# Gating one step ahead, taps behind the key chains, context's parts first: a reordering in a two-layer diffusion trunk

## The chip, the cores and the metric

The kernel runs on one core of a Trainium2 chip. A core has TensorE (PE: matmuls, and the loads of their weights, PEld), VectorE (DVE), ScalarE (ACT), GpSimd (POOL) and SyncE (SP, which here only issues DMAs). The metric is the device time of one execution in microseconds (us); lower is better.

## The reference, cut to what matters

A stream of 256 latent tokens and a prefix of 256 context tokens, width 1024, pass through two layers. All is float32. What the change touches is the first half of a layer, the token mixing:

```python
h = modulate(rmsnorm(x, norm1_g[l]), sh1, sc1)           # and hc likewise for the context
p = h @ w_in[l]                                          # GLU | q k v | gates, one projection
# (a) convolution branch
u = a * sigmoid(g)                                       # a, g: halves of the GLU columns
u = silu(layernorm(dwconv1d(u, conv_dw, conv_dw_b)))     # depthwise, 31 taps, 512 channels
y_conv = u @ w_conv_out
# (b) attention: 8 heads of 64; q, k of latents are rotated (rope);
#     each latent reads a window of the 4 x 64 grid (with a learned bias) and all context keys;
#     context tokens read context tokens only
y_attn = merge_heads(attention(q, k, v, k_ctx, v_ctx, rpb)) @ w_na_out
# (c) gates
x = x + g1 * ((sigmoid(gc) * y_conv + sigmoid(ga) * y_attn) @ w_out)
```

The second half is a gated MLP with a convolution of width 3. In the second (last) layer the context gives only keys and values.

## The kernel before

Activations lie with channels on the 128 partitions and tokens along the free axis: 512 columns in the first layer (256 latents, 256 context), 256 in the last. A matmul in full float32 precision is made of three: weights and activations are each split into a high part in a faster format (float32r) and the rest, and high x high, high x low, low x high are summed (`mm3`, L197 to L199). A `group` is one output tile of 128 channels: 8 input tiles x 3 = 24 matmuls of 512 columns in the first layer. Its weights come by one DMA of 512 KB on SP's queue, are split by ACT (the high part, L216), and get their low part either from ACT (L217) and an accumulating DMA of POOL (L218), or from DVE (L168).

The order of the work is written by hand as the order of the calls; a planner then orders each engine's queue, taking what is ready by its own estimate of durations, earlier calls first. `tc.issue_after(i)` keeps what is called inside behind `i` on the same engine. Beside the main order run *side* generators. `group` calls `slot()` in its middle and at its end, and each slot lets every side generator do one step:

- `conv_run` issues `rate` taps of the depthwise convolution. A tap (L673; L671 for a channel tile's first) is one DVE instruction over 128 channels and all columns, `cb = u * w + cb`. There are 4 channel tiles x 31 taps; a tile's taps can start once its GLU is done (`glu`: tanh on ACT, L691, then the product on DVE, L693). If `after[0]` is set, taps called later stand behind that instruction on DVE.
- `Attention.run` makes a step of the attention every few slots: products of queries and keys (L495), scores (DVE, L516: bias and row maximum; it sets `after[0]`), exponential and division (ACT, L519 and L522; DVE, L521), the turning of the probabilities (PE, L561; ACT copies, L564 and L567) and their product with the values (PE, L578; ACT and DVE, L595 and L596).
- later `ada_dots` (L304): products of the modulation weights on DVE, with weights by DMA into memory that the attention had used before.

The heads go in four pairs, j = 0 to 3. `qk(j)` makes the queries' and keys' groups of a pair; behind each, a chain of DVE and ACT rotates the latents' part (L859 to L869) and splits all parts into high (ACT, L881) and low (DVE, L882). `glu_groups(j)` makes the two groups of channel tile j of the GLU. In the first layer they alternate:

```python
qk(0)
...
for j in range(1, 4):
    glu_groups(j)
    qk(j)
    rate[0] = 3
```

and then gates (one group each) are made while attention is still busy, at most five. PSUM has four banks for groups (`main`), two (`sc`) and one and one (`pt`, `po`) for the attention. After the attention comes the LayerNorm of the convolution (`layer_norm`: what is left of the taps, five a slot, then sums L949 to L951 and a matmul, L955), the other gates, the two branch projections with their merge (L993, L998 to L1001), and the output projection.

Of the kernel before, what the change touches and what calls it, by code (L numbers as in the profile page):

```python
# [19 lines left out]
S = 256  # L20
GW = 64
# [32 lines left out]
def trunk(ctx: ExitStack, tc: tile.TileContext, xt, cvec, crow, wall, wada, params, bias_t, rope_t, out):  # L54
    nc = tc.nc
    pe, act, dve, pool, sp = nc.tensor, nc.scalar, nc.vector, nc.gpsimd, nc.sync
# [11 lines left out]
    def nm(s):  # L68
        uid[0] += 1
        return f"{s}_{uid[0]}"  # L70
# [18 lines left out]
    def add_side(gen):  # L89
        side.append(gen)  # L90
# [541 lines left out]
    for l in range(DEPTH):  # L632
        last = l == DEPTH - 1
        NS = 1 if last else 2
        T = NS * S
        ALL = slice(0, T)

        with ExitStack() if last else start as e1a:
# [59 lines left out]
            def in_group(t, c, tag="main"):  # L698
                return group(psum(tag), unit8(l, U_IN + t), *h1, c)

            def glu_groups(j):
                pa = in_group(T_GLU + 2 * (j - 1), ALL)
                pg = in_group(T_GLU + 2 * (j - 1) + 1, ALL)
                copied = None if last else att.ahead(j - 2)
                with tc.issue_after(copied.ins) if copied else ExitStack():
                    glu(j, pa, pg)

# [5 lines left out]
            with ExitStack() as e1b:  # L713
# [5 lines left out]
                def keep_v(t, ps):  # L719
                    if t > 1:  # L720
                        act.copy(halves(V[t - 2]), back(ps))
                        return
                    v = tmp()
                    act.copy(halves(v), back(ps))
                    for b in range(NB_):
                        for r in range(2):
                            at = r * GW + BASE[b]
                            sp.dma_start(VW[2 * t + r :: ROWS, b], v[at : at + WC])  # L728
# [108 lines left out]
                    glu_groups(1)  # L837

                conv = conv_run()
                rate[0] = 3 if last else 2.0  # L840
                add_side(conv)

                def qk(j):

                    att.ahead(j - 2)
                    bt = eb.tile([P, 5, NS_ // 2], F32, tag="bias", bufs=2 if last else 1, name=nm("bias"))
                    both = []
                    for what in range(2):
# [10 lines left out]
                        dve.tensor_tensor(part(r1[:, LAT]), lat, part(rope[:, 0, :]), ALU.mult)  # L859
                        dve.stream_shuffle(part(r2[:, LAT]), lat, SWAP16)  # L860
                        dve.tensor_tensor(r2[:, LAT], r2[:, LAT], rope[:, 1, :], ALU.mult)
                        if what == 0:
                            rq = tmp()
                            dve.tensor_tensor(
                                rq[:, LAT].rearrange("p (b r c) -> p b r c", b=NB_, r=ROWS),
                                blocks(r1[:, LAT]), blocks(r2[:, LAT]), ALU.add,
                            )
                        else:
                            dve.tensor_tensor(r1[:, LAT], r1[:, LAT], r2[:, LAT], ALU.add)  # L869
                        f = eb.tile([P, 2, KN if what else w], F32R, tag="qk"[what], bufs=2, name=nm("qk"))  # L870
                        if what == 0:
                            to = [([f[:, a, LAT] for a in range(2)], rq[:, LAT])]
                            if T > S:
                                to.append(([f[:, a, CTX] for a in range(2)], ctx_))
                        else:
                            rv_ = r1[:, LAT].rearrange("p (r c) -> p r c", r=ROWS)
                            to = [([f[:, a, KCTX] for a in range(2)], ctx_)]
                            for d, c in ((slice(0, KL), slice(GW - TC, GW)), (slice(KX, KN), slice(0, TC))):
                                to.append(([f[:, a, d].rearrange("p (c r) -> p r c", r=ROWS) for a in range(2)], rv_[:, :, c]))
                        for (hi, lo), src in to:  # L880
                            act.activation(hi, src, AF.Identity, scale=sc)  # L881
                            end = dve.scalar_tensor_tensor(lo, src, sc, hi.bitcast(F32), ALU.mult, ALU.subtract)  # L882
                        both.append(f)
                    att.pair(j, *both, bt, end)

                if l == 0:
                    for t in range(4):
                        keep_v(t, pv[t])
                    qk(0)
                    arun = att.run()  # L890
                    add_side(arun)
                    for j in range(1, 4):
                        glu_groups(j)
                        qk(j)
                        rate[0] = 3
                else:
                    glu_groups(2)
                    rate[0] = 3
                    wvs = [wunit(l, U_V + uu) for uu in range(4)]
                    for half in range(2):  # L900
                        pv = {t: psum() for t in (2 * half, 2 * half + 1)}
                        for k in range(KD):
                            v_tile(pv, wvs[k // 2], k, pv)
                            if k % 2:
                                slot()
                        for t, p in pv.items():
                            keep_v(t, p)
                    qk(0)
                    glu_groups(3)
                    arun = att.run()  # L910
                n = 0
                if last:
                    add_side(arun)
                    for j in range(1, 4):
                        gate(ea, n)
                        n += 1
                        qk(j)
                while att.busy() and n < (14 if last else 5):
                    gate(ea, n)
                    n += 1  # L920
                while att.busy():
# [435 lines left out]
```

## Time and profile before

| | |
|---|---|
| median of 3 runs | 1056.0 us (1055.9 to 1057.1) |
| the profiled execution | 1054.6 us, its span 1052.8 us |
| PE busy | 1032.4 us (98%) |
| DVE busy | 893.2 us (85%) |
| ACT busy | 565.6 us (54%) |
| POOL busy | 43.7 us (4%) |
| granted clock of TensorE | 0.997 of full speed |

The profile is of one execution. Times of rows are from the first instruction's start; "busy" of PE is modelled from pipelined matmuls. A row of waits says which engine's instruction waited for which, the total, how many times and the longest. A row of the timeline has the start, the duration, the engine and the line, the operation, what it writes and reads, how many instructions are merged, and in brackets the idle time before it and what ended that.

### The profile page before, as it was taken

What the parts mean: (1) busy time and instruction counts of PE and PEld (TensorE: products, weight loads), DVE (VectorE), ACT (ScalarE), POOL (GpSimd) and SP (SyncE); (2) the same over time, 40 slices, a digit from 0 to 9 for tenths busy, and PEclk for the clock granted to TensorE, in tenths of its full rate; (3) what the DMA queues carried; (4) which work ended last, traced back from release to release, by engine and by line L of the source; (5) the groups of instructions that cost most, each with busy time, mean ns of one, the idle gap of its engine ahead of it and who ended that gap; (6) DMA issues with size and microseconds to landing.
All of it is one profiled execution on the core that took longest, in us unless ns stands there. A gap on an engine that the chain in (4) does not pass through costs nothing.

```text
span 1052.8 us, 17991 instructions
## 1 busy us (share of the span) xinstructions
PE 1032.4 (98%) x6886; PEld 932.9 (89%) x6886; DVE 893.2 (85%) x1608; ACT 565.6 (54%) x921; POOL 43.7 (4%) x59
## 2 busy tenths in 40 slices
PE   9999999999999999999999999999999999999997
PEld 7787788888889988888888889999889999999996
DVE  6568899999998787878788888799899988988883
ACT  4458768545434644444444223545777666766652
POOL 1111110011000000000000000000000000000000
PEclk9999999999999999999999999999999999999998
DMA  9989674888945345454545887556734485666781
GB/s 374 305 221 229 156 181 121 258 255 236 305 146 177 104 140 160 140 164 143 166 145 160 301 289 249 180 189 209 208 123 135 161 292 176 193 201 199 221 283 57
DMA packets 59511, 209.26 MB, mean 199 GB/s; under 512 B 7201, under 2 KB 7457, under 8 KB 59425
## 3 DMA queue, kind: packets, MB, share of 16 engines
q1 hardware_dynamic: 54384, 190.77, 55.3%
q0 software_dynamic: 4752, 17.30, 8.7%
q8 instruction: 54, 0.88, 0.3%
q14 instruction: 33, 0.26, 0.1%
q10 hardware_dynamic: 288, 0.04, 0.0%
HBM read 187.63 MB, written 1.05 MB: 179 GB/s over the span
## 4 chain that ended last, share of the span: by engine, by line
PE 68%; DVE 17%; ACT 5%; DMA 4%; issue 3%; SPq 1%; DVEq 0%; ACTq 0%
PE main L197 20%; PE main L198 20%; PE main L199 20%; DVE cb L673 6%; PE main L736 4%; DVE wlo L168 3%; DMA raw<-in_wall 2%; DVE t L304 2%; DMA own<-in_wada 1%; SPq L728 1%; PE sc L197 1%; PE sc L199 1%; PE sc L198 1%; DVE qk L882 1%; ACT pp L519 1%
## 5 line engine op out<-in xcount | busy, mean ns | idle before, releaser
L197 PE MATMUL main<-h,whi 128*128 128x256 f32 (+1 forms) x1328 | 433.1, 326 | 1.2 <-DVE qk L882 1.2
L198 PE MATMUL main<-h,whi 128*128 128x256 f32 (+1 forms) x1328 | 430.2, 324 | 0.9 <-DVE h L1001 0.7
L199 PE MATMUL main<-h,wlo 128*128 128x256 f32 (+1 forms) x1328 | 429.9, 324 | 1.2 <-DVE wlo L168 1.1
L167 ACT CAST whi<-raw 128x1024 fp32r<-128x1024 f32 (+1 forms) x211 | 218.3, 1039 | 234.8 <-PE main L198 173.6
L168 DVE TENSOR_TENSOR wlo<-raw,whi 128x1024 fp32r<-128x1024 f32 (+1 forms) x211 | 253.6, 1208 | 67.2 <-ACT whi L167 66.4
L197 PEld LDWEIGHTS main<-h,whi 128*128 128x128 f32 x1328 | 252.8, 190 | 22.0 <-issue 1.3
L199 PEld LDWEIGHTS main<-h,wlo 128*128 128x128 f32 x1328 | 252.5, 190 | 18.5 <-DVE wlo L168 1.8
L198 PEld LDWEIGHTS main<-h,whi 128*128 128x128 f32 x1328 | 252.7, 190 | 18.3 <-DVE h L1001 1.0
L304 DVE CUSTOM_DVE_ANT_0 t<-own,sb,par 128x1024 bf16<-128x1024 f32 x120 | 151.8, 1282 | 6.8 <-DMA own<-in_wada 6.8
L673 DVE SCALAR_TENSOR_TENSOR cb<-u,par,cb 128x512 f32<-128x512 f32 (+1 forms) x240 | 144.7, 620 | 2.8
L198 PE MATMUL main<-fl,whi 128*128 128x256 f32 (+1 forms) x396 | 122.8, 310 | 0.0
L197 PE MATMUL main<-fh,whi 128*128 128x256 f32 (+1 forms) x396 | 122.8, 310 | 0.0
L199 PE MATMUL main<-fh,wlo 128*128 128x256 f32 (+1 forms) x396 | 122.5, 310 | 0.0
L197 PEld LDWEIGHTS main<-fh,whi 128*128 128x128 f32 x396 | 75.6, 191 | 3.8 <-ACT fh L1095 0.2
L198 PEld LDWEIGHTS main<-fl,whi 128*128 128x128 f32 x396 | 75.6, 191 | 3.7 <-DVE fl L1096 0.2
L199 PEld LDWEIGHTS main<-fh,wlo 128*128 128x128 f32 x396 | 75.5, 191 | 3.6
L216 ACT CAST whi<-raw 128x1024 fp32r<-128x1024 f32 x33 | 34.6, 1049 | 36.0 <-PE main L198 30.5
L404 ACT ACTIVATE h<-t,mod 128x256 fp32r<-128x256 f32 x56 | 25.2, 503 | 34.8 <-DVE t L403 34.3
L218 POOL DMA_DIRECT2D wlo<-raw x33 | 28.9, 877 | 258.9 <-ACT wlo L217 107.6
L736 PE MATMUL main<-whi,h 128*128 128x512 f32 x128 | 38.5, 386 | 0.2
L1105 ACT ACTIVATE t<-t 128x512 f32<-128x512 f32 x22 | 13.9, 632 | 41.3 <-DVE t L1074 41.3
L217 ACT ACTIVATE wlo<-whi 128x1024 fp32r<-128x1024 f32 x33 | 35.0, 1061 | 0.5
(214 smaller groups left out, 1268.8 us busy)
## 6 DMA issues: line engine op xcount, KB each, us to landing
raw<-in_wall SPq DMA_DIRECT2D x240, 512.0 KB, 4.3
own<-in_wada SPq DMA_DIRECT2D x72, 512.0 KB, 4.7
wlo<-raw POOLq DMA_DIRECT2D x33, 512.0 KB, 5.4
raw<-in_wada SPq DMA_DIRECT2D x16, 512.0 KB, 5.8
bias<-in_bias_t SPq DMA_DIRECT2D x8, 520.0 KB, 5.3
row<-in_wada SPq DMA_DIRECT2D x8, 512.0 KB, 5.1
sb<-in_crow SPq DMA_DIRECT2D x5, 512.0 KB, 4.8
x<-in_xt SPq DMA_DIRECT2D x4, 512.0 KB, 5.1
```

The source lines that it names most:

```text
L167: act.copy(hi[:, c], r[:, c])
L168: dve.tensor_tensor(lo[:, c], r[:, c], hi[:, c].bitcast(F32), ALU.subtract)
L197: pe.matmul(ps, w[0], order(xh), start=start, stop=False)
L198: pe.matmul(ps, w[0], order(xl), start=False, stop=False)
L199: pe.matmul(ps, w[1], order(xh), start=False, stop=stop)
L216: act.copy(hi, r)
L217: act.mul(lo, hi.bitcast(F32), -1.0)
L218: pool.dma_start(lo, r, accum_op=ALU.add)
L304: dve.tensor_tensor_reduce(tmp().bitcast(BF16), r, v, 1.0, pr(l, BADA + n, 1), ALU.mult, ALU.add, mods[l][:, n, s : s + 1])
L404: high = act.activation(hi[:, c], y[:, c], AF.Identity, bias=b)
L673: dve.scalar_tensor_tensor(cb[j], src, w, cb[j], ALU.mult, ALU.add)
L736: mm = pe.matmul(pv[t], h1[n == 1][k][:, c], runs(w[n == 2][:, b]), start=k + n == 0, stop=k == KD - 1 and n == 2)
```

## The change

In the first layer, `glu_groups(1)` is called ahead of `qk(0)`, and `glu_groups(j + 1)` ahead of `qk(j)`; a gate takes the place of the missing one ahead of `qk(3)`. The taps' rate goes from 2, then 3, to a schedule: 4 in the first GLU groups, 2 in queries and keys, 3 and then 4 in GLU groups, 4 behind the last pair. After each `qk` in the first layer `after[0]` is the last low part of the keys, so taps called from then on stand behind the chain. Up to eight gates, not five, may run while the attention is busy. In both layers the context's parts of queries and keys are split ahead of the rest of the rotation, and the two window parts of the keys change places. The core of the diff:

```diff
 def glu_groups(j):
     pa = in_group(T_GLU + 2 * (j - 1), ALL)
+    if not last and j > 1:
+        rate[0] = 4.0
     pg = in_group(T_GLU + 2 * (j - 1) + 1, ALL)
-    copied = None if last else att.ahead(j - 2)
+    copied = None if last else att.ahead(j - 3)
     with tc.issue_after(copied.ins) if copied else ExitStack():
         glu(j, pa, pg)
...
-rate[0] = 3 if last else 2.0
+rate[0] = 3.0
...
+def parts(f, d, src, sc, view=lambda a: a):
+    hi, lo = (view(f[:, a, d]) for a in range(2))
+    act.activation(hi, src, AF.Identity, scale=sc)
+    return dve.scalar_tensor_tensor(lo, src, sc, hi.bitcast(F32), ALU.mult, ALU.subtract)
 
 def qk(j):
     att.ahead(j - 2)
+    if not last:
+        rate[0] = 2.0
...
         dve.stream_shuffle(part(r2[:, LAT]), lat, SWAP16)
+        f = eb.tile([P, 2, KN if what else w], F32R, tag="qk"[what], bufs=2, name=nm("qk"))
+        if ctx_ is not None:
+            parts(f, KCTX if what else CTX, ctx_, sc)
         dve.tensor_tensor(r2[:, LAT], r2[:, LAT], rope[:, 1, :], ALU.mult)
...
         if what == 0:
-            to = [([f[:, a, LAT] for a in range(2)], rq[:, LAT])]
-            if T > S:
-                to.append(([f[:, a, CTX] for a in range(2)], ctx_))
+            end = parts(f, LAT, rq[:, LAT], sc)
         else:
             rv_ = r1[:, LAT].rearrange("p (r c) -> p r c", r=ROWS)
-            to = [([f[:, a, KCTX] for a in range(2)], ctx_)]
-            for d, c in ((slice(0, KL), slice(GW - TC, GW)), (slice(KX, KN), slice(0, TC))):
-                to.append(([f[:, a, d].rearrange("p (c r) -> p r c", r=ROWS) for a in range(2)], rv_[:, :, c]))
-        for (hi, lo), src in to:
-            act.activation(hi, src, AF.Identity, scale=sc)
-            end = dve.scalar_tensor_tensor(lo, src, sc, hi.bitcast(F32), ALU.mult, ALU.subtract)
+            for d, c in ((slice(KX, KN), slice(0, TC)), (slice(0, KL), slice(GW - TC, GW))):
+                end = parts(f, d, rv_[:, :, c], sc, lambda a: a.rearrange("p (c r) -> p r c", r=ROWS))
+        if not last:
+            after[0] = end
     att.pair(j, *both, bt, end)
+    rate[0] = 4.0 if j == 3 and not last else 3.0
...
 if l == 0:
...
+    rate[0] = 4.0
+    glu_groups(1)
     qk(0)
     arun = att.run()
     add_side(arun)
-    for j in range(1, 4):
-        glu_groups(j)
+    for j in range(1, 3):
+        glu_groups(j + 1)
         qk(j)
-        rate[0] = 3
...
-    for j in range(1, 4):
-        gate(ea, n)
-        n += 1
-        qk(j)
-while att.busy() and n < (14 if last else 5):
+for j in range(1 if last else 3, 4):
+    if True:
+        gate(ea, n)
+        n += 1
+        qk(j)
+while att.busy() and n < (14 if last else 8):
```

More of the change, by code (lines that the diff above doesn't have):

```diff
@@ L869, in qk @@
                             dve.tensor_tensor(r1[:, LAT], r1[:, LAT], r2[:, LAT], ALU.add)
-                        f = eb.tile([P, 2, KN if what else w], F32R, tag="qk"[what], bufs=2, name=nm("qk"))
                         if what == 0:
-                            to = [([f[:, a, LAT] for a in range(2)], rq[:, LAT])]
-                            if T > S:
-                                to.append(([f[:, a, CTX] for a in range(2)], ctx_))
+                            end = parts(f, LAT, rq[:, LAT], sc)
                         else:
                             rv_ = r1[:, LAT].rearrange("p (r c) -> p r c", r=ROWS)
-                            to = [([f[:, a, KCTX] for a in range(2)], ctx_)]
-                            for d, c in ((slice(0, KL), slice(GW - TC, GW)), (slice(KX, KN), slice(0, TC))):
-                                to.append(([f[:, a, d].rearrange("p (c r) -> p r c", r=ROWS) for a in range(2)], rv_[:, :, c]))
-                        for (hi, lo), src in to:
-                            act.activation(hi, src, AF.Identity, scale=sc)
-                            end = dve.scalar_tensor_tensor(lo, src, sc, hi.bitcast(F32), ALU.mult, ALU.subtract)
+                            for d, c in ((slice(KX, KN), slice(0, TC)), (slice(0, KL), slice(GW - TC, GW))):
+                                end = parts(f, d, rv_[:, :, c], sc, lambda a: a.rearrange("p (c r) -> p r c", r=ROWS))
+                        if not last:
+                            after[0] = end
                         both.append(f)
                     att.pair(j, *both, bt, end)
+                    rate[0] = 4.0 if j == 3 and not last else 3.0
                 if l == 0:
```

## The prediction

> **What bounds the kernel now.** First the page: busy time of each engine.
>
> ```profile
> span 1052.8 us, 17991 instructions
> PE 1032.4 (98%) x6886; PEld 932.9 (89%) x6886; DVE 893.2 (85%) x1608; ACT 565.6 (54%) x921; POOL 43.7 (4%) x59
> ```
>
> TensorE (PE) is idle for 1052.8 - 1032.4 = 20.4 us in all. A change that only reorders work can win no more than the part of this that lies where it acts. So the second view is what PE waited for, once in the first layer's mixing stage (60 to 300 us) and once in the second layer's (700 to 900).
>
> ```profile
> PE sc L495 <- ACT pT L567: 1.7, 1, 1.7
> PE po L955 <- DVE ss L951: 1.0, 1, 1.0
> PE sc L495 <- ACT qk L881: 0.9, 1, 0.9
> PE main L198 <- DVE h L1001: 0.7, 1, 0.7
> PE sc L495 <- DVE qk L882: 0.6, 1, 0.6
> PE pt L495 <- ACT pT L564: 0.3, 1, 0.3
> PE pt L561 <- ACT pp L522: 0.3, 1, 0.3
> ...
> PE pt L370 <- DVE ss L356: 1.8, 2, 1.0
> PE main L197 <- DVE qk L882: 1.2, 2, 0.6
> ```
>
> Columns: total us, times, longest. The first seven rows are the first layer: 1.7 + 0.9 + 0.6 + 0.3 + 0.3 = 3.8 us in the attention (L495 is query times key, L561 the turning of the probabilities), 1.0 at the convolution's LayerNorm, 0.7 at the branch merge. The last two are the second layer's.
>
> Third, busy time by stretch, to see who is behind these waits.
>
> ```profile
> 57.00:77.00 20.00, 20.00 (x94) 17.24 (x92) 16.39 (x32) 9.92 (x16) 3.46 (x4) 1.00 0.88 210
> 77.00:88.50 11.50, 11.50 (x60) 9.99 (x60) 6.80 (x21) 11.36 (x20) 1.73 (x2) 1.00 1.00 272
> 214.00:293.00 79.00, 78.34 (x369) 68.33 (x368) 73.52 (x118) 36.31 (x46) 8.14 (x8) 1.00 0.86 256
> 746.00:822.00 76.00, 73.64 (x699) 67.58 (x697) 74.28 (x179) 54.71 (x121) 2.31 (x2) 1.00 0.51 157
> ```
>
> Columns: PE, PE loads, DVE, ACT, POOL, then PE's granted clock. From 57 to 88.5 DVE is idle for 3.6 + 4.7 us, just ahead of the first long wait; from 746 to 822 it is busy for 98%. PE needs 20.00 / 94 = 0.213 us a matmul, so a group of 24 takes 5.1 us. Fourth, DVE's order around the first wait, and how many taps (L673) ran by then.
>
> ```profile
> 57.00:77.00 20.00, 11.21 (x15) 1.00 0.88 210
> 77.00:92.30 15.30, 5.79 (x8) 1.00 0.96 271
> ...
> 73.02 1.54 DVE L673 SCALAR_TENSOR_TENSOR cb<-u,par,cb 128x512 f32<-128x512 f32 x2
> 77.84 0.60 DVE L516 CUSTOM_DVE_ANT_0 sc<-sc,bias 128x416 f32<-128x416 f32 x1 [3.29 <-PE sc L495]
> 80.60 0.69 DVE L693 SCALAR_TENSOR_TENSOR u<-t,main 128x512 f32<-128x512 f32 x1 [1.55 <-ACT t L691]
> 83.56 0.16 DVE L521 RECIPROCAL ri<-sm 128x1 f32<-128x1 f32 x1 [2.27 <-ACT pp L519]
> 84.79 1.53 DVE L673 SCALAR_TENSOR_TENSOR cb<-u,par,cb 128x512 f32<-128x512 f32 x2
> 92.40 0.42 DVE L859 TENSOR_TENSOR t<-main,rope 128x256 f32<-128x256 f32 x1
> 93.09 0.74 DVE L673 SCALAR_TENSOR_TENSOR cb<-u,par,cb 128x512 f32<-128x512 f32 x1
> 94.74 1.54 DVE L673 SCALAR_TENSOR_TENSOR cb<-u,par,cb 128x512 f32<-128x512 f32 x2
> 96.20 0.81 DVE L882 SCALAR_TENSOR_TENSOR qk<-t,qk 128x160 fp32r<-128x160 f32 x2
> 96.91 1.55 DVE L673 SCALAR_TENSOR_TENSOR cb<-u,par,cb 128x512 f32<-128x512 f32 x2
> ```
>
> The chain of the second pair's keys runs from 92.40 (L859) to 97.0 (second L882). With the tap at L671, 1 + 15 + 8 = 24 taps precede it, which is what the code's slots give up to this point. So the three at 93.09 and 94.74 belong to slots behind the chain and stand inside it: 3 x 0.66 = 2.0 us, while PE waits 0.9 + 0.6.
>
> **The change part by part.**
>
> *Gated channels one step ahead.* Groups before: Q0 K0 G1 Q1 K1 G2 Q2 K2 G3 Q3 K3, then gates (G is two groups). After: G1 Q0 K0 G2 Q1 K1 G3 Q2 K2 gate Q3 K3. The first product of a pair comes two groups (10.2 us) later, and counting slots the attention ends in the seventh gate, not the fifth: two groups later too. The same groups run, so PE's work is unchanged and the later end costs only what must wait for it. On SP and POOL the weight loads of G1 and their accumulations change places with those of Q0 and K0, as many and as large; PE has no idle from 57 to 88.5 above, so the exchange costs 0 (bounds 0 and the few tenths that the small L495 waits show). Rates 4, 2, 3, 4 instead of 2 give, by the slots, 38 taps ahead of the first scores (16 before) and 52 ahead of the second (30 before), all 124 by the attention's end (102 before). Taps in one row cost:
>
> ```profile
> 135.65 4.06 DVE L673 SCALAR_TENSOR_TENSOR cb<-u,par,cb 128x512 f32<-128x512 f32 x6
> 181.20 3.90 DVE L673 SCALAR_TENSOR_TENSOR cb<-u,par,cb 128x512 f32<-128x512 f32 x5
> ```
>
> 0.66 us each where two channels alternate (the first row; a second channel had begun), 0.78 where one channel's taps follow each other. 22 more taps are at most 22 x 0.78 = 17.2 us, with the gating (0.6) 17.8. They have 10.2 us more, and the idle 3.3 at 77.84: DVE comes up to 17.8 - 13.5 = 4.3 us late to the first scores, 1.6 if all alternate. What covers it is ACT:
>
> ```profile
> 81.53 1.28 ACT L519 ACT_TABLE_LOAD   x1
> 82.83 0.61 ACT L519 ACTIVATE pp<-sc,mx 128x416 f32<-128x416 f32 x1
> ```
>
> The first exponential starts at 82.83 behind weight splits and a table load, though its score was ready by 78.5: 4.3 us. I take this lateness as absorbed; if that cover is short, every us goes on to the later scores (rival A).
>
> [...]
>
> *Taps behind the chains.* Every tap of a slot behind a pair now follows its last key part. Of those standing in chains this moves three at pair 1. The chain ends 2.0 us earlier; the wait of 0.9 + 0.6 is wholly ahead of that: -1.5 (bounds -1.5 and 0). But six taps stand behind it and ahead of the scores, where three stood: 4.7 instead of 2.3 us, so the scores start no sooner than now, and PE, 1.5 us ahead, meets their probabilities at L561:
>
> ```profile
> 103.26 1.29 ACT L522 ACTIVATE pp<-pp,ri 128x416 f32<-128x416 f32 x2
> 104.61 0.27 PE L561 MATMUL pt<-ident,pp 64*128 64x64 f32 x1 [0.25 <-ACT pp L522]
> ```
>
> Here PE already waits 0.25. The bounds: scores go ahead of these six taps (wait gone, -0.25), or the scores are 4.7 - 2.3 - 2.0 = 0.4 to 0.8 us later by the clock of the shifted order, which costs 1.5 + 0.8 = +2.3. Before, the taps at 96.91 went ahead of the scores, so I lean to the upper end: a wait of 1.6 in place of 0.25, +1.35. The small wait at L495 on pT (0.3) lies behind this one and falls away: -0.27.
>
> *Rate 2 in queries and keys, context first.* The largest wait, 1.7, is for the copies L567:
>
> ```profile
> 125.32 0.81 ACT L881 ACTIVATE qk<-t 128x160 fp32r<-128x160 f32 x2 [1.58 <-DVE t L869]
> 125.91 1.07 ACT L216 CAST whi<-raw 128x1024 fp32r<-128x1024 f32 x1
> 127.02 1.06 ACT L217 ACTIVATE wlo<-whi 128x1024 fp32r<-128x1024 f32 x1
> 127.98 1.05 ACT L567 COPY pT<-sc 128x512 f32<-128x512 f32 x2
> ```
>
> ACT stood 1.58 us for DVE's key chain, and the copies queue behind it. From the context's scores to this chain's end there are now 8 taps instead of 12 and one that jumped in: 5 x 0.66 = 3.3 us less. The 1.58 goes, and of PE's 1.7 I leave 0.3: -1.4 (bounds -1.7 and 0, if ACT splits weights in the time won). Then the later, small waits: +0.1 for the last context scores, which come behind taps of rate 4.
>
> *In the second layer* only the order of parts changes. It frees the bank behind the 1.2 us of waits (L197 on L882) by about two DVE steps. But DVE is busy 98% from 746 to 822 and PE then waits for it (L370, 1.0 of that row's 1.8): the gain comes back as a longer wait there. I take 0 (bounds -1.2 and 0).
>
> *The end of the attention.* All taps are then done, so the LayerNorm's sums no longer wait for tap 124:
>
> ```profile
> 186.88 2.46 SPq L154 DMA_DIRECT2D own<-in_wada  x4
> 196.55 1.28 DVE L304 CUSTOM_DVE_ANT_0 t<-own,sb,par 128x1024 bf16<-128x1024 f32 x1 [0.60 <-DMA own<-in_wada]
> 212.27 0.69 DVE L951 TENSOR_TENSOR ss<-ss,cb 128x512 f32<-128x512 f32 x1
> ```
>
> The 1.0 us at L955 goes: -0.97 (bounds -1.0 and 0). Against it: the modulation products L304 begin about 10 us later, since their buffers take the attention's memory, and now no taps fill DVE while the first loads land (9.6 us from issue to use). From 214 to 293 DVE is idle for 79.0 - 73.5 = 5.5 us. It loses 10.2 us of time and sheds nine taps that now run among the products (5.9) and a split of weights (1.1): 5.5 - 3.2 = 2.3 us remain, so I leave the merge's wait (0.7) as it is (bounds 0 and +3.2).
>
> *Sum:* -1.5 + 1.35 - 0.27 - 1.4 + 0.1 + 0 - 0.97 = -2.7 us. The profiled execution took 1054.6 us (span 1052.8), 1.4 below the median of the runs, 1056.0. So the profile would give 1051.9, the runs 1053.3.
>
> **The rivals.**
>
> A, slower: DVE's backlog is not absorbed. Place: the first scores; it decides once DVE is over the covered 4.3 us late there, or once ACT's splits shift so that nothing is covered. Then 4.3 us go on to L561 of pair 1, and the key chain of pair 2 is late as well (the -1.4 is lost): -2.7 + 4.3 + 1.4 = +3.0, 1059.0. For it: the estimate stands at the edge. Against: 4.7 us of idle DVE at 77 to 88.5.
>
> B, no change: DVE sets the pace, and waits only move. L561 takes the full +2.3, half of the -1.4 is lost: -2.7 + 0.95 + 0.7 = -1.05, 1055.0. For it: the second layer shows just that. That the edge behind the chain does little also belongs here: beside the three taps of pair 1 few stood in chains, and the taps of the keys' own slots are not bound by it.
>
> C, much faster: all waits named go, 3.8 + 1.0 + 0.7 and 1.2 in the second layer: -6.7, 1049.3. For it: alternating taps shorten DVE's work; against: the 98%.
>
> **How the numbers follow.** 0.2% (2.1 us) is about what a measurement of this kernel can tell from no change. Forecast 0.42, its own range 1052 to 1054.5; A 0.18; B 0.28; C 0.12. Faster: C and four fifths of the forecast, 0.45. Same: B, the rest of the forecast and a little of A, 0.37. Slower: 0.18. The range 1050.5 to 1058.5 cuts off the outer halves of A and C, some 0.15 to 0.2.
>
> **What would show it.** Right: some 38 L673 or L671 ahead of the first L516, no tap between L869 and the last key part's L882; the waits L495 on L881 and L882 gone, L495 on pT L567 under 0.5, L955 gone; L561 on pp grown. Wrong: a PE wait of over 2 us at L561, or one at a group's start on the gating's u (L693); an idle DVE of over 5 us around 200 followed by a wait on L1001 of over 1.5; or the wait at L370 in the second layer shorter than now, which would make its order of parts count.

## The result and the profile after

The changed kernel takes 1068.9 us (median; 1067.0 to 1070.2), the kernel before 1056.3 beside it: ratio 1.0118, interval 1.0103 to 1.0133. It is 12.6 us slower, where 2.7 less was forecast. The profiled execution took 1067.0 us, and its page begins

```profile
span 1065.2 us, 17996 instructions
PE 1037.3 (97%) x6886; PEld 934.9 (88%) x6886; DVE 895.9 (84%) x1608; ACT 564.9 (53%) x921; POOL 43.4 (4%) x59
```

DVE, ACT and POOL do as much as before (893.2, 565.6, 43.7). PE's idle time went from 20.4 us to 27.9, and its busy time rose by 4.9 with the same 6886 matmuls: some of them ran slower. First the waits of PE, from 60 to 300 us and from 700 to 900 (total us, times, longest):

```profile
PE pt L561 <- ACT pp L522: 4.0, 3, 2.1
PE pt L561 <- ACT pp L540: 1.4, 1, 1.4
PE sc L495 <- ACT qk L847: 0.8, 1, 0.8
PE sc L561 <- ACT pp L522: 0.6, 1, 0.6
PE sc L495 <- ACT pT L564: 0.6, 1, 0.6
PE sc L561 <- ACT pp L540: 0.4, 1, 0.4
PE sc L561 <- ACT pp L535: 0.2, 1, 0.2
...
PE pt L370 <- DVE ss L356: 1.8, 2, 1.0
PE sc L495 <- ACT pT L564: 1.5, 3, 0.7
PE main L199 <- DVE wlo L168: 1.4, 2, 0.9
```

Two of the waits that the change aimed at are gone: L495 on pT L567 (1.7) and L955 (1.0). Of the third, for the key chain of pair 1 (0.9 + 0.6, now L847), 0.8 is left. In their place stand 4.6 us at L561 on the latents' probabilities (L522) and 2.0 on the context's (L535, L540). In the second layer the bank's 1.2 us (L197) are gone, and L495 and L199 wait 2.9 in place of 1.3. Then the stretches (columns as in the prediction; the sixth number is PE's granted clock):

```profile
57.00:77.00 20.00, 20.00 (x95) 17.50 (x94) 17.50 (x27) 8.95 (x11) 3.46 (x4) 1.00 0.80 174
77.00:97.00 20.00, 20.00 (x100) 17.16 (x99) 15.78 (x29) 11.57 (x15) 3.45 (x4) 1.00 0.95 247
121.00:125.00 4.00, 4.00 (x46) 3.56 (x42) 3.30 (x6) 3.52 (x8) 0.86 (x1) 0.57 0.34 113
188.00:197.00 9.00, 6.70 (x61) 4.36 (x60) 7.82 (x15) 8.97 (x25) 0.86 (x1) 0.81 0.00 0
224.00:303.00 79.00, 77.79 (x366) 67.61 (x365) 73.71 (x118) 36.18 (x46) 8.14 (x8) 1.00 0.88 263
```

DVE is still idle for 2.5 + 4.2 us between 57 and 97, although taps were waiting. And twice, from 121.4 and from 193.1, PE ran at half clock for 3.4 us (granted clock 0.51 from 121.4 to 124.8, 0.50 from 193.1 to 196.5). At the end of the first stretch L495's matmuls of 256 columns start 0.21 us apart (124.27, 124.48, 124.69), behind it 0.11 (124.89, 125.00, 125.11). By that I estimate that each such stretch costs up to half its length, 1.7 us: all of it only if PE has matmuls without a pause. Before, there was none: the clock is 1.00 up to 1045 us, and PE is busy for 0.6 us after that.

**Where the 12.6 us went.** For every two successive matmuls I take the time between their starts less what the first needs for its columns (0.213 us for 512, as in the prediction; at least 27 ns, what 64 take at that rate). The sum over a stretch is the time that PE lost there, by waits or by a slow clock. The stretches are cut by matmul work already done, so each holds the same work in every kernel: from 55 to 112 us of work (first scores, pairs 0 and 1), to 140 (pair 2), to 185 (end of the attention), to 215 (LayerNorm), to 290 (branches and merge), to 325 (output projection, first norm, start of the feed-forward), and the rest. "Dots" are the L304 that stand on DVE directly ahead of that norm's first column sum (L378). All from the profiled executions, the half clock's length inside the kernel (up to PE's last matmuls) too; the medians and ratios are those of the timed runs. The kernels ran in five sets, each beside the kernel before, whose medians were 1055.8 to 1057.1; between sets the ratios compare better. A row is one execution and not always one near the median: that of `beforeparts` took 1062.5 us, the longest of its ten, that of `shiftonly` 1061.2, the shortest of its six. In `fill` the columns of the added matmuls (40 rows of 128 in the trace, 2.1 us at that rate) count as work.

| kernel | 55-112 | -140 | -185 | -215 | -290 | -325 | rest | at half clock | dots | median us | ratio to before |
|---|---|---|---|---|---|---|---|---|---|---|---|
| before | 2.2 | 2.8 | 1.3 | 2.7 | 2.4 | 3.8 | 38.9 | 0 | 1 | 1056.3 | |
| after | 8.2 | 0.3 | 7.5 | 1.5 | 3.1 | 6.2 | 39.9 | 6.8 | 3 | 1068.9 | 1.0118 |
| noedge | 3.3 | 1.0 | 4.9 | 1.5 | 3.8 | 6.3 | 38.2 | 6.8 | 3 | 1060.6 | 1.0033 |
| tail3 | 8.3 | 0.4 | 1.1 | 2.5 | 3.4 | 13.9 | 39.7 | 17.0 | 5 | 1068.7 | 1.0104 |
| oldrate | 5.2 | 1.9 | 5.2 | 0.8 | 4.2 | 13.4 | 39.9 | 17.0 | 5 | 1069.8 | 1.0118 |
| beforeparts | 2.5 | 6.6 | 0.9 | 2.0 | 7.4 | 3.8 | 38.9 | 13.6 | 1 | 1058.2 | 1.0007 |
| edgeonly | 5.5 | 1.4 | 3.3 | 2.0 | 2.4 | 3.8 | 39.6 | 3.4 | 1 | 1059.3 | 1.0027 |
| shiftonly | 0.0 | 1.8 | 3.6 | 0.8 | 3.9 | 12.5 | 38.7 | 6.8 | 5 | 1064.5 | 1.0076 |
| noedge_tail3 | 3.1 | 0.9 | 1.4 | 1.2 | 3.4 | 13.6 | 39.3 | 10.2 | 5 | 1063.3 | 1.0068 |
| tail3_dots | 7.8 | 0.5 | 1.0 | 2.1 | 2.7 | 6.3 | 41.1 | 6.8 | 3 | 1061.1 | 1.0042 |
| edge_late | 4.7 | 1.2 | 7.6 | 1.5 | 3.0 | 6.2 | 39.5 | 3.4 | 3 | 1066.2 | 1.0086 |
| shift_dots | 0.1 | 1.8 | 3.7 | 0.8 | 5.5 | 3.8 | 39.4 | 0 | 1 | 1056.1 | 1.0000 |
| repaired | 3.6 | 0.9 | 1.4 | 1.9 | 7.4 | 3.8 | 40.1 | 3.4 | 1 | 1060.1 | 1.0030 |
| repaired_late | 6.9 | 0.1 | 0.9 | 2.8 | 8.5 | 3.8 | 40.6 | 13.6 | 1 | 1063.5 | 1.0054 |
| fill | 6.4 | 1.0 | 8.6 | 1.5 | 2.4 | 7.6 | 41.4 | 10.2 | 3 | 1071.3 | 1.0126 |
| after_dots | 8.4 | 0.5 | 8.4 | 1.5 | 3.6 | 4.5 | 39.6 | 13.6 | 1 | 1066.5 | 1.0085 |
| repaired2 | 3.2 | 1.0 | 1.5 | 1.6 | 2.7 | 4.5 | 40.3 | 0 | 1 | 1055.3 | 0.9985 |
| shift_best | 0.1 | 1.8 | 3.7 | 0.8 | 3.2 | 4.8 | 40.2 | 0 | 1 | 1055.2 | 0.9979 |

After less before, row by row: +6.0, -2.5, +6.2, -1.2, +0.7, +2.4, +1.0, in all 12.6. So two gains as forecast and three losses: at the first scores, at the end of the attention, and at the first norm.

*The first scores*, DVE and ACT after the last low part of pair 0's keys (L848, the former L882):

```profile
86.57 1.07 DVE L848 SCALAR_TENSOR_TENSOR qk<-t,qk 128x160 fp32r<-128x160 f32 x2 [0.69 <-ACT qk L847]
87.55 0.72 DVE L673 SCALAR_TENSOR_TENSOR cb<-u,par,cb 128x512 f32<-128x512 f32 x1
88.19 0.53 DVE L671 TENSOR_SCALAR cb<-u,par 128x512 f32<-128x512 f32 x1
88.64 8.03 DVE L673 SCALAR_TENSOR_TENSOR cb<-u,par,cb 128x512 f32<-128x512 f32 x12
96.59 0.59 DVE L516 CUSTOM_DVE_ANT_0 sc<-sc,bias 128x416 f32<-128x416 f32 x1
...
97.28 0.61 ACT L519 ACTIVATE pp<-sc,mx 128x416 f32<-128x416 f32 x1 [4.71 <-DVE mx L516]
...
102.36 0.27 PE L561 MATMUL pt<-ident,pp 64*128 64x64 f32 x1 [2.12 <-ACT pp L522]
```

Fourteen taps, 9.0 us, stand in one block between the chain and the scores, while DVE had 6.7 us idle before (six of the 14 run earlier without the tie, below). ACT idles 4.71 us before the first exponential, and PE then 2.12.

*The end of the attention*, DVE ahead of the last context scores (L530):

```profile
176.50 5.47 DVE L673 SCALAR_TENSOR_TENSOR cb<-u,par,cb 128x512 f32<-128x512 f32 x7
181.89 1.22 DVE L168 TENSOR_TENSOR wlo<-raw,whi 128x1024 fp32r<-128x1024 f32 x1
183.02 1.53 DVE L673 SCALAR_TENSOR_TENSOR cb<-u,par,cb 128x512 f32<-128x512 f32 x2
...
184.81 0.74 DVE L673 SCALAR_TENSOR_TENSOR cb<-u,par,cb 128x512 f32<-128x512 f32 x1
185.47 1.28 DVE L530 TENSOR_REDUCE mx<-sc 128x2 f32<-128x512 f32 x2
```

Ten taps and a weight split, and then the scores from 185.47 on. In the kernel before there are five taps behind the split, and DVE is idle ahead of the scores:

```profile
166.29 3.90 DVE L673 SCALAR_TENSOR_TENSOR cb<-u,par,cb 128x512 f32<-128x512 f32 x5
170.41 0.42 DVE L596 TENSOR_TENSOR ol<-po,oh 128x256 fp32r<-128x256 f32 x1 [0.22 <-ACT oh L595]
170.75 1.28 DVE L530 TENSOR_REDUCE mx<-sc 128x2 f32<-128x512 f32 x2
```

After, PE turns the context's probabilities from 189 to 194, with the waits at L561 on L535 and L540 between, and falls to half clock at 193.1 (0.50 up to 196.5).

*The first norm.* DVE in the kernel before, then after:

```profile
322.69 1.28 DVE L304 CUSTOM_DVE_ANT_0 t<-own,sb,par 128x1024 bf16<-128x1024 f32 x1
323.89 0.16 DVE L378 TENSOR_SCALAR red<-pt 128x2 f32<-128x2 f32 x1
```

```profile
332.26 1.28 DVE L304 CUSTOM_DVE_ANT_0 t<-own,sb,par 128x1024 bf16<-128x1024 f32 x1
333.46 1.28 DVE L304 CUSTOM_DVE_ANT_0 t<-own,sb,par 128x1024 bf16<-128x1024 f32 x1
334.67 1.28 DVE L304 CUSTOM_DVE_ANT_0 t<-own,sb,par 128x1024 bf16<-128x1024 f32 x1
335.88 0.15 DVE L378 TENSOR_SCALAR red<-pt 128x2 f32<-128x2 f32 x1
```

The dots run one pair every few slots; what is not done by then is issued in one piece ahead of the norm. After, with the attention two groups longer, there are three instead of one.

### The profile page after: what moved, and what is told of

Same layout as the page of the kernel before. It is cut to its first block, busy times and chain, and to the rows that moved or that the text cites. A ratio compares the mean times of both kernels' runs of the same rounds, so it can differ in the third digit from the quotient of the medians.

```text
span 1065.2 us, 17996 instructions
## 1 busy us (share of the span) xinstructions
PE 1037.3 (97%) x6886; PEld 934.9 (88%) x6886; DVE 895.9 (84%) x1608; ACT 564.9 (53%) x921; POOL 43.4 (4%) x59
## 4 chain that ended last, share of the span: by engine, by line
PE 70%; DVE 17%; ACT 5%; DMA 4%; issue 3%; SPq 1%; DVEq 0%; POOL 0%; ACTq 0%; POOLq 0%
PE main L197 20%; PE main L198 20%; PE main L199 20%; DVE cb L673 5%; PE main L738 4%; DVE wlo L168 3%; DMA raw<-in_wall 2%; DVE t L304 2%; SPq L730 1%; ACT pp L519 1%; ACT whi L167 1%; PE sc L199 1%; PE sc L198 1%; PE sc L197 1%; PE po L578 1%
## 5 line engine op out<-in xcount | busy, mean ns | idle before, releaser
L197 PE MATMUL main<-h,whi 128*128 128x256 f32 (+1 forms) x1328 | 432.9, 326 | 0.6 <-ACT h L1010 0.5
L199 PE MATMUL main<-h,wlo 128*128 128x256 f32 (+1 forms) x1328 | 429.9, 324 | 1.7 <-DVE wlo L168 1.4
L197 PEld LDWEIGHTS main<-h,whi 128*128 128x128 f32 x1328 | 252.8, 190 | 21.2 <-issue 1.9
L199 PEld LDWEIGHTS main<-h,wlo 128*128 128x128 f32 x1328 | 252.5, 190 | 19.1 <-DVE wlo L168 2.1
L304 DVE CUSTOM_DVE_ANT_0 t<-own,sb,par 128x1024 bf16<-128x1024 f32 x120 | 151.0, 1277 | 13.3 <-DMA own<-in_wada 13.2
L197 PE MATMUL main<-fh,whi 128*128 128x256 f32 (+1 forms) x396 | 122.8, 310 | 0.0
L199 PE MATMUL main<-fh,wlo 128*128 128x256 f32 (+1 forms) x396 | 122.5, 310 | 0.0
L197 PEld LDWEIGHTS main<-fh,whi 128*128 128x128 f32 x396 | 75.6, 191 | 3.8 <-ACT fh L1105 0.2
L199 PEld LDWEIGHTS main<-fh,wlo 128*128 128x128 f32 x396 | 75.5, 191 | 3.5
L1115 ACT ACTIVATE t<-t 128x512 f32<-128x512 f32 x22 | 13.9, 631 | 41.0 <-DVE t L1084 41.0
```

Of the source, the lines that this page charges most:

```text
L197: pe.matmul(ps, w[0], order(xh), start=start, stop=False)
L199: pe.matmul(ps, w[1], order(xh), start=False, stop=stop)
L304: dve.tensor_tensor_reduce(tmp().bitcast(BF16), r, v, 1.0, pr(l, BADA + n, 1), ALU.mult, ALU.add, mods[l][:, n, s : s + 1])
```

## The experiments

**The tie.** `noedge`, the changed kernel without it:

```diff
-if not last:
-    after[0] = end
```

> The changed kernel without the line that sets after[0] behind the key chain; all else as changed. Theory one (DVE's queue: taps that may not run ahead of the key chain of pair 0 leave DVE idle and then stand, 14 of them, ahead of the first scores): in DVE's order 30 instead of 24 taps run ahead of that chain's end and 8 instead of 14 between it and the first scores, so the scores come some 4 us earlier, PE's wait of 2.1 us at L561 of pair 0 goes, and with it the stretch at a lower granted clock around 117 us; 3 to 5 us faster than the changed kernel, about 1064. Theory two (the shift of the gating by one step costs, whatever the taps' order): no change, 1067 to 1070. Theory three (the edge is what helps and the rest harms): slower than the changed kernel by the 1.4 us that the key chain's wait cost before.

1060.6 us, 8.3 less than with the tie (9.0 by the ratios), more than theory one's 3 to 5. DVE then:

```profile
87.48 5.38 DVE L673 SCALAR_TENSOR_TENSOR cb<-u,par,cb 128x512 f32<-128x512 f32 x8
92.78 0.58 DVE L516 CUSTOM_DVE_ANT_0 sc<-sc,bias 128x416 f32<-128x416 f32 x1
```

Eight taps instead of 14 in front of the scores, which start 3.8 us sooner; six others ran in and between the chains. PE's waits from 60 to 130 are then those for the key chain of pair 1 again:

```profile
PE sc L495 <- ACT qk L847: 1.3, 1, 1.3
PE sc L495 <- DVE qk L848: 0.5, 1, 0.5
```

That is the wait which the tie was to take away: it costs 1.8 us, and the tie more. Nor does the tie take all of it: 0.8 us is left in the changed kernel, where three taps stand inside the key chain of pair 1 (105.53 to 110.3), as many as before:

```profile
105.86 0.75 DVE L673 SCALAR_TENSOR_TENSOR cb<-u,par,cb 128x512 f32<-128x512 f32 x1
...
106.87 0.74 DVE L673 SCALAR_TENSOR_TENSOR cb<-u,par,cb 128x512 f32<-128x512 f32 x1
...
107.86 0.75 DVE L673 SCALAR_TENSOR_TENSOR cb<-u,par,cb 128x512 f32<-128x512 f32 x1
```

They are behind the last low part of the queries, and nothing ties them to the keys' own.

`edgeonly`, the kernel before with the tie alone:

```diff
+if not last:
+    after[0] = end
 both.append(f)
```

> The kernel before with nothing of the change but the tie of the taps (in the first layer every tap stands behind the last low part of the last query or key chain). Theory one, the tie costs because taps that were to run between and ahead of a chain's pieces are pushed into a block between the last key chain and the first scores (14 taps there in the changed kernel, 9.0 us): here no block forms, because before's rate of 2 and its gating order bring only 16 taps ahead of the first scores with and without the tie; so 1055 to 1058 us. Rival, the tie costs by itself some 8 us, as between the changed kernel and the one without the tie: 1062 to 1066 us.

1059.3 us (1.0015 to 1.004): neither number. Ahead of the first scores eight taps stand in one piece, where three did, but DVE is through with them before PE brings the scores (it is then idle for 0.74 us). At pair 1 five stand where three did, and the scores start at 101.25 and not at 99.16:

```profile
97.44 3.90 DVE L673 SCALAR_TENSOR_TENSOR cb<-u,par,cb 128x512 f32<-128x512 f32 x5
101.25 0.59 DVE L516 CUSTOM_DVE_ANT_0 sc<-sc,bias 128x416 f32<-128x416 f32 x1
```

3.3 us more are lost at pairs 0 and 1 and 2.0 at the end of the attention, against 1.4 and 0.7 gained. So the tie costs by itself, by some 3 us, and by 8 in the company of the higher rates and the early gating.

`edge_late`, the changed kernel with the tie from pair 1 on:

```diff
-if not last:
+if not last and j > 0:
     after[0] = end
```

> The changed kernel with the tie of the taps kept for pairs 1 to 3 and left out for pair 0. The taps then run within and between pair 0's chains (30 instead of 24 ahead of the end of its key chain) and 8 instead of 14 stand between that chain and the first scores. Theory one, the first loss (the waits of the transposes at 102 and 117 to 120, 4.0 us with the rest of L561, and a stretch at half clock) is of this block alone: 1062 to 1065 us. Rival, the block only moves to the next pair, whose tie makes one of its own: 1067 to 1070 us.

1066.2, between the two. The wait of 2.1 us at pair 0 is gone, and PE waits at pair 1:

```profile
PE pt L561 <- ACT pp L522: 1.9, 2, 1.5
PE sc L495 <- ACT qk L847: 1.0, 1, 1.0
PE sc L561 <- ACT pp L522: 0.6, 1, 0.6
```

The rival is partly right: at pair 1, too, the tie pushes taps in front of the scores (five where `noedge` has three; the scores start at 111.49 and not at 109.95).

**The rates.** `tail3`, the changed kernel with a rate of 3 behind the last pair too:

```diff
-rate[0] = 4.0 if j == 3 and not last else 3.0
+rate[0] = 3.0
```

> The changed kernel with rate 3 instead of 4 behind the last pair. Theory one: the 16 taps of two gates that stand ahead of the last context scores become 12; those scores start some 2.5 us earlier, the waits at L561 on L540 and L535 around 190 us (2.0 us in all) and the lower clock there go; 3 to 5 us faster than the changed kernel, about 1064. Theory two: no change.

1068.7, theory two's number, though theory one holds at its place: the end of the attention is cured (7.5 to 1.1) and the sum is not better. By the code the LayerNorm raises the dots' pace once the taps are done, and now taps are left; five dots are left ahead of the norm, and 13.9 us are lost there instead of 6.2, with 10.2 us at half clock.

`oldrate`, the changed kernel with the rates of before, 2 and then 3:

```diff
-    rate[0] = 4.0                     # in glu_groups
...
-    rate[0] = 2.0                     # in qk
...
-rate[0] = 4.0 if j == 3 and not last else 3.0
+rate[0] = 3.0 if j > 0 or last else 2.0
...
-rate[0] = 4.0
+rate[0] = 2.0
 glu_groups(1)
```

> The changed kernel with the rates of the kernel before (2 up to the second pair's keys, then 3). Kept: gating one step ahead, taps behind the chains, context's parts first. Theory one (it is the number of taps ahead of the scores, by the rates): 24 taps ahead of the first scores instead of 38, 12 ahead of the last context scores; both losses go, 1054 to 1058. Theory two (the shift of gating costs by itself): 1062 or more.

1069.8: the higher rates are not the cause as a whole. Theory one is right in part, for the first two losses shrink (8.2 to 5.2, 7.5 to 5.2), but five dots are left here too, and the third grows from 6.2 to 13.4.

`noedge_tail3`, the edits of `noedge` and `tail3` together:

> The changed kernel without the tie and with a tap rate of 3, not 4, behind the last pair. Theory one: the losses at the first scores (about 8 us with the tie) and at the end of the attention (about 6) are then both gone, and what is left is the third, behind the attention: the rows' dots of the modulation start later and leave the first units of the feed-forward waiting (a wait of about 5 us on the low part of a weight, with half clock behind it, as in the kernel with the rate alone changed); 1058 to 1062 us. Rival, that third loss was a consequence of the tie: 1053 to 1056 us.

1063.3, above both ranges, but with the losses that theory one named: the first two are all but gone (3.1 and 1.4), the third is not. The wait is the same in the four kernels that have five dots; here that of `shiftonly`, from 285 to 360 us:

```profile
PE sc L199 <- DVE wlo L168: 5.4, 1, 5.4
```

**The order of parts.** `beforeparts`, the kernel before with only the context's parts first and the windows exchanged (the change's `parts` and its calls in `qk`, nothing else of it):

```diff
+f = eb.tile([P, 2, KN if what else w], F32R, tag="qk"[what], ...)
+if ctx_ is not None:
+    parts(f, KCTX if what else CTX, ctx_, sc)
 dve.tensor_tensor(r2[:, LAT], r2[:, LAT], rope[:, 1, :], ALU.mult)
```

> The kernel before with the order of parts alone (context's parts first, the two window parts of the keys exchanged), in both layers. The prediction's step: the bank waits of the second layer (1.2 us, L197 on the low parts) go, but the wait for the LayerNorm's sums behind them grows by as much, 1056 +- 1. If the bank were the limit: 1055. If the order hurts the rotation chain: over 1057.

1058.2 (1054.7 to 1062.5; ratio 0.9988 to 1.0026): the median is over 1057, but this is nothing that can be told from no change, the second layer included.

**The early gating.** `shiftonly`, the kernel before with the groups' order of the change, and gates that follow from it:

```diff
-copied = None if last else att.ahead(j - 2)
+copied = None if last else att.ahead(j - 3)
...
+glu_groups(1)
 qk(0)
...
-for j in range(1, 4):
-    glu_groups(j)
+for j in range(1, 3):
+    glu_groups(j + 1)
     qk(j)
```

> Of the change only the gating one step ahead (with the gate projections that follow from it): before's tap rates, order of parts and no tie. 24 taps are queued on DVE ahead of the first scores instead of 16, and the last pair's context scores stand behind 92 instead of 90. Theory one, the loss comes with taps that stand ahead of scores: 8 more taps of 0.66 to 0.78 are 5.3 to 6.2 us on DVE at the first scores, of which 4 lie in DVE's idle time of 77 to 88; 1056 to 1059 us. Rival, the shift is itself the loss (the attention ends later in PE's order and everything behind it follows): 1061 to 1066 us. Second rival, the shift alone takes waits away: 1052 to 1055 us.

1064.5 us: the rival's number, and it was not the 8 taps ahead of the scores, for nothing is lost there (0.0, the best of all kernels). The loss is at the first norm, with five dots: 8.7 us more than before, while the other stretches together lose 1.5 less. `shift_dots` is the same with the dots' pace raised:

```diff
-pace[0] = 0.5       # behind the attention
+pace[0] = 0.9
...
-pace[0] = 0.0 if last else 0.3      # in the branches
+pace[0] = 0.0 if last else 0.45
```

> The gating one step ahead alone, with the modulation's dots behind the attention paced faster (0.9 a slot instead of 0.5, and 0.45 instead of 0.3 in the branches), so that one dot stands directly ahead of the first norm's column sums, as before, and not four to six. Theory one, the shift costs only by those dots (8.7 us lost at the start of the feed-forward against the kernel before): 1054 to 1058 us. Rival, the dots take from taps and LayerNorm what they give to the norm: 1060 to 1065 us.

1056.1, ratio 1.0000 (0.9986 to 1.0014): 8.4 us (8.0 by the ratios) come back by two numbers, and DVE has as much to do. The early gating costs nothing but the dots that it leaves over.

**The dots in the changed kernel.** `tail3_dots` (`tail3` with the first pace at 0.9) and `after_dots` (the changed kernel with 0.7 and 0.35):

> The changed kernel with a tap rate of 3 behind the last pair, and the dots of the modulation behind the attention paced 0.9 a slot instead of 0.5, so that they are done before the norm ahead of the feed-forward needs DVE. Theory one, the 8.9 us that this kernel lost at the start of the feed-forward come from dots that pile up there: the wait of 5.4 us on a weight's low part and the half clock behind it are gone, 1059 to 1064 us. Rival, the pile is not of the dots (or they delay the taps and LayerNorm instead): 1066 to 1070 us as without the new pace.

> The changed kernel with only the dots' pace changed (0.7 a slot instead of 0.5 behind the attention, 0.35 instead of 0.3 in the branches), so that one dot and not three stands directly ahead of the first norm's column sums on DVE. Theory one, by the kernels so far one dot there goes with 3.8 us lost at the start of the feed-forward, three with 6.2, five with 12.5 to 13.9: 2.4 us less than the changed kernel, less up to 1.5 that the dots may cost at the branches: 1066 to 1068 us. Rival, the dots cost at the branches all they give (as 3.7 us at the output projection in the repaired kernel): 1068.5 to 1071 us.

1061.1 with three dots instead of five, 7.6 us less than `tail3` (6.5 by the ratios); 1066.5 with one instead of three, 2.3 less than the changed kernel (3.5). Over all 18 kernels one dot ahead of the norm goes with 3.8 to 4.8 us lost there, three with 6.2 to 7.6, five with 12.5 to 13.9.

**All three losses taken out.** `repaired` (no tie, rate 3 at the end, paces 0.9 and 0.45) and `repaired_late` (the same with the tie from pair 1 on):

> The changed kernel with all three losses taken out: no tie, a tap rate of 3 behind the last pair, the faster pace of the dots. Theory one, the three add up: of the kernel without the tie and with the rate (1063.3) the 9.8 us of the feed-forward's start go, 1052.5 to 1056.5 us. Rival, the dots' new place costs elsewhere or the half clock takes another stretch: 1057 to 1062 us.

> The repaired kernel with the tie of the taps for pairs 1 to 3. Theory one, the tie hurts at pair 0 alone, where 14 taps are queued with nothing else for DVE to do ahead of the first scores; here the wait for the key chain of pair 2 goes (0.5 us) and the LayerNorm is no later: within 1.5 us of the repaired kernel. Rival, every tie moves taps behind a chain and ahead of scores, and pairs 1 to 3 pay too: 3 to 6 us slower than the repaired kernel.

1060.1 and 1063.5, the rivals' numbers. In `repaired` the first norm is as before (3.8), but the loss from 215 to 290 is 7.4, of which one wait at the output projection:

```profile
PE main L197 <- DVE t L1006: 3.7, 1, 3.7
```

L1006 is a step of the merge (before, L999): dots at that pace stand between the merges. The tie costs 3.4 us more here (2.5 by the ratios), in the pairs that keep it. `repaired2` has 0.38 in place of 0.45:

> The repaired kernel with a pace of 0.38 in the branches instead of 0.45; one dot still stands ahead of the first norm. Theory one, the repaired kernel's missing 4 us are the wait of 3.7 us at the output projection and its half clock, made by dots that run between the merges: with fewer of them there it comes to 1055 to 1058 us. Rival, the wait has another cause and stays: 1059 to 1061 us.

1055.3: the wait is gone (2.7 lost there), 0.9985 of before (0.9976 to 0.9993). `shift_best`, the early gating alone with 1.0 and 0.38:

> The gating one step ahead alone with dots paced 1.0 behind the attention and 0.38 in the branches: one dot ahead of the first norm, as with 0.9 and 0.45, and fewer dots between the merges. Theory one, of the 3.1 us that the kernel with 0.9 and 0.45 lost at the branches against the kernel before, 1 to 3 come back: 1052.5 to 1055.5 us, faster than before. Rival, the loss there is not of the pace: 1055.5 to 1057 us.

1055.2, 0.9979 (0.997 to 0.9988). These two beat both kernels, the one before by 1.7 and 1.8 us. They differ by rates, order of parts and the first pace, which together are worth nothing that shows.

**The half clock.** `fill`, the changed kernel with matmuls of the identity in PE's waits:

```diff
+j = its[0][0]
+if self.l == 0 and what == LAT and j < 2:
+    for _ in range(((0, 10), (3, 7))[j][n]):
+        pe.matmul(..., ident, ident, start=True, stop=True)
```

> The changed kernel with matmuls of the identity (128 columns, some 0.21 us each by the 0.43 us of L578's 256 columns) put where TensorE waits at the turns of pairs 0 and 1: ten ahead of the second half of pair 0's transposes (a wait of 2.1 us), three and seven ahead of pair 1's two halves (0.6 and 1.5 us). Their results are overwritten. They take the place of waits and change no order on the other engines. Theory one, the stretch at half clock behind those waits (3.4 us at 121.4, worth 1.7 us) is started by the waits: it is gone from the trace, PEclk is 1.00 in 112 to 140, and the time is 1.0 to 2.0 us less than the changed kernel's, 1066.5 to 1068. Rival, the small transposes or the time of day set it and not the waits: the stretch stays, and the time is unchanged or up to 0.6 us more, 1068.5 to 1069.5.

```profile
121.00:125.00 4.00, 3.48 (x52) 2.60 (x52) 3.54 (x5) 3.97 (x8) 0.86 (x1) 1.00 0.60 229
...
180.00:200.00 20.00, 17.88 (x121) 13.96 (x121) 18.08 (x30) 13.15 (x37) 0.86 (x1) 0.83 0.36 94
```

The clock is 1.00 where it was 0.57, as theory one said. The time is 1071.3 (1067.6 to 1071.9), above both ranges: the twenty added matmuls take 5.1 us, more than the waits they fill (2.1 + 0.6 + 1.5), and at the end of the attention, where nothing was filled, this execution had 6.8 us at half clock and not 3.4, and 3.4 more at 350. Nor does one execution show that the filling kept the clock. `edge_late` has the waits at pair 1 unfilled (0.63 and 1.50 us), and its clock stays at 1.00 over them:

```profile
114.00:126.00 12.00, 9.08 (x93) 7.42 (x93) 9.81 (x19) 10.42 (x28) 0.86 (x1) 1.00 0.61 155
```

That a filled wait keeps the clock fits this run but is not shown, and that it saves time is not either.

## Why the prediction was wrong

- **Gating one step ahead: PE's work unchanged, "the later end costs only what must wait for it".** True, and the bill was not made. I followed the dots to 293 us and bounded their cost at the merge (0 to +3.2; it came to +0.7). That dots left over are issued in one piece ahead of the first norm I did not look for: 2.4 us here, 8.4 with the rates of before.
- **22 more taps ahead of the first scores.** The count is right (38 in the trace, 16 before). The step that failed is the next: "I take this lateness as absorbed" by ACT's 4.3 us, and DVE's idle time as available. The tie forbids just that. The scores start 18.75 us later than before (96.59 and 77.84), where 10.2 for the two groups and at most 4.3 were allowed for, and ACT, which was to cover it, stands idle for 4.71 us. The stretch lost 6.0 us more than before, in place of 0. The taps alternated between channels (12 in 8.03 us, 0.67 each), so the price of one was not the matter.
- **Taps behind the chains: -1.5 + 1.35.** I looked at pair 1, where three taps stood in the chain, and wrote in rival B that the tie "does little". Three stand there still, and 0.8 of the 1.5 us is left. I did not count the six taps that ran inside pair 0's two chains before (62.90 to 70.67); with the tie alone (`edgeonly`) none does. The tie is the largest single cause: 8.3 us less without it. A wait at L561 did take the place of that at L495, but of 4.6 us in all and from pair 0 on.
- **Rate 2 in queries and keys, L495 on L567: -1.4.** Right: the wait is gone, -2.5 from 112 to 140. **LayerNorm, -0.97:** right, -1.2. **Second layer, 0:** right, though L370, where I saw the gain come back, still waits 1.8 us; L495 and L199 took it. `beforeparts` shows no gain.
- **Last context scores behind taps of rate 4: +0.1.** Mis-sized: +6.2, of which at most 1.7 by the clock. With rate 3 it is gone (`tail3`); but `oldrate` and `shiftonly`, which have that rate there as well, lose 5.2 and 3.7, and that was not followed up.
- **The clock.** I took 1.00 throughout. Two stretches of 3.4 us at half speed are at most 3.4 us of the 12.6. How much of it shows in the time stays open: `tail3`, `tail3_dots` and `after_dots` do the same work up to the last pair, were at half clock twice and not once at the first scores (6.8 us, not 3.4), and lost 8.3, 7.8 and 8.4 us there, where the changed kernel lost 8.2.
- **Rival A** had the place and the mechanism, DVE's backlog at the first scores, with a price of one wait. The price was several such waits with the clock behind them, and two more backlogs of the same kind further on.

What stays open: the losses do not add up exactly. Without the tie also the end of the attention is 2.6 us better, and the half clock takes other stretches in other kernels. How much of the tie's 8.3 us is the first block and how much that later effect was not separated.

## What to carry to other kernels

Work that may fill idle time is worth most while it is free to go early: tie it behind a chain, and it piles up in front of whatever is next on that engine. When a stage is lengthened or moved, follow its helpers to where the last of them is forced out (here the dots ahead of a norm, some 130 us behind the attention), for there the cost comes in one piece. And a reordering that "costs nothing" should be tried with the paces tuned again, for the same order was 8 us slower or 1.8 us faster by two numbers.

## What the runs showed of the hardware

In the changed kernel PE's clock fell to half twice, for 3.4 us each (0.51 and 0.50 over the two stretches), and in every kernel of the table the sum at half clock is a multiple of 3.4. In `tail3` it fell some 2.9 us into the wait of 5.4, by the mean clock: the wait began at 339.3, and 0.93 from 325 to 345 is 2.8 us at half. In `shiftonly`, with the same wait, 0.74 from 334 to 347 is 6.8 us at half; in `repaired`, with the wait of 3.7, 0.81 from 290 to 299 is 3.4. In the changed kernel the waits ahead of it are shorter, 1.49 us at the longest (L561 at 119.61) ahead of the stretch at 121.4 and 1.36 (L561 at 191.97) ahead of that at 193.1. The 3.4 us ahead of each:

```profile
118.00:121.40 3.40, 1.52 (x22) 1.01 (x20) 3.29 (x8) 3.18 (x8) 0.00 (x0) 1.00 0.71 239
...
189.70:193.10 3.40, 1.62 (x18) 0.94 (x18) 3.33 (x8) 3.40 (x13) 0.00 (x0) 1.00 0.00 0
```

PE was busy for 1.52 and 1.62 us of 3.40, less than half. But how busy PE was does not settle it. In the first row here, again the changed kernel, it was busy for only 1.14 us, and the clock was 1.00 then and up to 121.4; in the second, `noedge` ahead of its stretch at 186.0, for 2.37 us, and the clock fell:

```profile
100.00:103.40 3.40, 1.14 (x21) 0.80 (x18) 3.37 (x11) 3.40 (x9) 0.00 (x0) 1.00 0.84 282
...
182.60:186.00 3.40, 2.37 (x36) 1.53 (x36) 3.29 (x8) 3.40 (x12) 0.00 (x0) 1.00 0.00 0
```

At 103 `tail3`, `tail3_dots` and `after_dots`, with the same work up to there, did fall to half clock (17.0, 6.8 and 13.6 us of it in all, where the changed kernel had 6.8): the same work brought it on in one execution and not in another. The stretches lie at places that vary from kernel to kernel, and the runs of one kernel scatter (`noedge` 1056.6 to 1064.5 us, `shift_best` 1053.5 to 1056.3). What brings a stretch on, and what makes it 3.4 us long, these traces do not show. In the three stretches of 3.4 us that are shown here ahead of a slow one PE worked 45 to 70% of the time.
